# State-space parameters multiplied without zero blocks, placed on the block diagonal by ScalarE, with their last steps spread into the down projection

## Chip, cores and metric

One NeuronCore of a Trainium2 chip. The metric is the device time of one execution in microseconds, the median of several. Engines are named as in the profile: PE (TensorE matmul), PEld (its weight loads), DVE (VectorE), ACT (ScalarE), POOL (GpSimd), SP (SyncE, which here only issues DMAs).

## What is computed

Four transformer-like layers on 256 tokens of 1,024 features, in two blocks of two layers. Every layer is a token mixer and a feed-forward with a depthwise convolution. The third mixer holds a state-space part (S5) whose parameters are made on the chip. The reference, cut to what matters here:

```python
def _conv_ffn(xn, w_up, conv_w, conv_b, w_down):       # layers 1 and 2
    a, gval = jnp.split(xn @ w_up, 2, axis=-1)         # 2 x 2816 columns
    a = depthwise_conv(a, conv_w, width=3) + conv_b
    return (jax.nn.gelu(a) * gval) @ w_down

def s5(u, a_re, a_im, log_dt, b_re, b_im, c_re, c_im, ...):   # in layer 3
    abar = exp((a_re + 1j * a_im) * exp(log_dt))       # 32 groups x 64 states
    bbar = (abar - 1) / (a_re + 1j * a_im) * b         # 32 x 64 x 16
    s_t  = abar * s_(t-1) + bbar @ u_t
    y_t  = Re(c @ s_t) + d * u_t
```

## The kernel before

Activations lie feature-major: a tile has 128 features in the partitions and 256 tokens in the columns. Every large product is made in three passes (`mm3`, L187 to L189): weights and activations are split into a high and a low part, and PE adds high x high, high x low and low x high. So each piece of weights (128x1024) is loaded by SP (`raw`), ACT makes its high part (`whi`, L170) and DVE its low part (`wlo`, L172). Four buffers each of raw, whi and wlo, and four PSUM banks, let them run ahead of PE.

A feed-forward (`ffn`, L514) is an up projection of 22 chunks and a down projection of 8 output tiles. A chunk is 48 matmuls of 256 columns: a tile of a and one of the gate. Behind each chunk stands a chain over four engines: DVE multiplies by the norm's factor (ag, L526), ACT and DVE make the convolution (L531, twice L539), ACT the activation (L541), POOL multiplies by the gate (cv, L542), ACT makes the high part (ah, L543) and POOL the low part (al, L544). The tile cv has two buffers, and ag three. The down projection takes 66 matmuls for an output tile, then DVE adds it to h (L569) and `feed` makes the next norm's operand. In the second feed-forward `feed` is `EdgeNorm.feed` (L582): for every tile POOL makes two sums of squares (L255 or L259 and L262; L585 to L591). PE sums them over the partitions with L275, in its order, after 53 matmuls of the next projection.

The second feed-forward also carries the parameters of the S5 part. `S5.prepare` is a generator that `ffn` gets as `side`; each `next(side)` issues one step, mostly for POOL, behind a chunk's al (L544). Its steps:

- angles, powers, sine and cosine (L659 to L699), on small tiles;
- `times` (L702): one complex product for each of the four powers of B and the four of C, each in two halves (real, imaginary) of three POOL operations (L707, L708, L709) on 128 x 512. A tile has 16 columns for each of its two groups of states, 32 in all, and half of them are zeros: the host has put B and C on a block diagonal (`blocks`);
- the kernel K: 128 small matmuls on PE (L726), then 32 transposes of B (L736), with copies by ACT (L729, L737);
- `turn` (L742): the table E by doubling, from 1 to 64 columns (L753 to L758 on POOL).

After the 22 chunks a loop issues what is left, so all steps are issued ahead of the down projection. The order on each engine is made by a scheduler that sorts by its own estimate of times, and every engine runs its instructions in that order. The parameters arrive by three DMAs from the ACT queue (L640, L643, L645), in the second mixer. In the program E is the tile [128, 2, 16, 64]; its columns 0 to 31 hold B at first, columns 32 to 63 C.

Of the kernel before, what the change touches and what calls it, by code (L numbers as in the profile page):

```python
# [98 lines left out]
def build(tc, A, O, stop=None):  # L99
# [3 lines left out]
    with es:  # L103
# [53 lines left out]
        class Piece:  # L157
            """columns of a weight chunk as high and low part"""
# [42 lines left out]
        def chunkA(src, X, nk=8):  # L201
            """[m 2][k][128] chunk: two feature tiles of X @ W, one bank."""
# [8 lines left out]
        def chunksA(srcs, X, nk=8, late=2, raw=None):  # L211
            """the same for several chunks, where the last operand tiles come late"""
# [23 lines left out]
        class Norm:  # L236
            """RMS norm of the rows of h, as h is made; its gain goes into the operand, 1/rms waits."""
# [30 lines left out]
        def sums(acc, nh, perm=False, more=None, tag="sm"):  # L268
            """token sums of acc over partitions and halves, as columns: [128, 2 (+2)]"""
# [20 lines left out]
        def spread(rs):  # L290
            """columns of token factors -> [128, 256], the same in every partition"""
# [82 lines left out]
        def chunkB(srcs, X, toks, nk=4, n=512, tag="mm"):  # L374
            """token-major: chunks [k][n]; one bank for each token tile"""
# [22 lines left out]
        def qk_head(l, j, X, rb, qkv):  # L398
            """tiles q_j, q_4+j, q_8+j, k_8+j, k_4+j, k_j; all but k_j in order of token parity"""
# [13 lines left out]
        def softmax_rows(s, n):  # L413
            """rows of s (SBUF) -> probabilities, in place"""
# [101 lines left out]
        def ffn(nm, win, cw, cb, wdown, act, shifts, feed, side=None):  # L516
# [6 lines left out]
            for i in range(NF):  # L523
# [21 lines left out]
                if side is not None:  # L545
                    with tc.issue_after(last.ins):
                        for _ in range(1 + (i + 1) % 2):
                            next(side, None)
            for _ in side or ():
                pass  # L550
# [13 lines left out]
            for m in range(8):  # L564
# [5 lines left out]
                feed(m)  # L570

# [60 lines left out]
        class S5:  # L632
            """y = Re(C s), s_t = a s_(t-1) + B~ u_t, four tokens to a step: over quads c of tokens
            s_c = a^4 s_(c-1) + w_c, w_c = sum_j a^(3-j) B~ u_(4c+j). In the frame that turns with the phase of a^4
            the recurrence has the real factor |a|^4: two real scans, z. Then
            y_(4c+j) = Re(C a^(j+1) s_(c-1)) + sum_(i<=j) K_(j-i) u_(4c+i), K_l = Re(C a^l B~)."""

            def __init__(self):
# [3 lines left out]
                self.Bm = self.E[:, :, :, 0:32]  # L642
                nc.scalar.dma_start(out=self.Bm, in_=A["s5_b"])  # L643
                self.C0 = self.E[:, :, :, 32:64]
                nc.scalar.dma_start(out=self.C0, in_=A["s5_c"])  # L645
# [4 lines left out]
            def prepare(self, lbp):  # L650
                """the parameters, in steps that go between other work"""
                P, Bm, C0, C, B, K = self.P, self.Bm, self.C0, self.C, self.B, self.K
# [46 lines left out]
                GS(C0[:, 1], C0[:, 1], -1.0, None, op0=ALU.mult)  # L699
                yield  # L700
                x = lambda c: c.unsqueeze(2).to_broadcast([128, 16, 32])

                def times(o, a, re, im, ops=(ALU.subtract, ALU.add)):
                    """o = a * (re + i im); o, a: real and imaginary [128, 16, 32]"""
                    for c, op in enumerate(ops):
                        tm = sp.tile([128, 512], F32, tag="t%d" % c, name="tm", bufs=1).rearrange("p (a b) -> p a b", a=16)
# [7 lines left out]
                for j in (2, 1, 0):  # L714
                    yield from times(b[j], b[j + 1], are, aim)
# [458 lines left out]
def prepare(inp):  # L1174
# [65 lines left out]
    def blocks(v):  # L1240
# [3 lines left out]
        for g in range(2):  # L1244
            o[g, :, :, g, :] = v[:, g].transpose(1, 0, 2)
# [41 lines left out]
```

## Time and profile before

| | us |
|---|---|
| median of 3 runs (1568.94 to 1570.26) | 1569.27 |
| span of the profiled execution | 1566.8 |
| PE busy | 1519.9 (97%) |
| DVE busy | 1066.2 (68%) |
| ACT busy | 779.6 (50%) |
| POOL busy | 613.3 (39%) |
| DMA, mean of 16 engines | 166 GB/s |

The only time of the profiled execution that is known is its span, from the first to the last instruction; the run's own time also holds what lies around it. PE is busy nearly everywhere, so the places where it is not are to be looked for in the slices and stretches. A busy share is a mean over four layers that are limited by different things.

### The profile page before, as it was taken

The page shows a single profiled execution, that of the slowest core. Times are in us where ns is not written, and L with a number is a line of the kernel's source. Part 1 is how long each engine was busy: PE and PEld are TensorE (multiplying, and loading weights), DVE is VectorE, ACT ScalarE, POOL GpSimd, SP SyncE. Part 2 cuts the span into 40 slices and gives each one's busy share as a digit, 9 for nine tenths or more (in the row PEclk, how much of TensorE's full clock was granted, in tenths as well). Part 3 has the DMA queues.
Part 4 walks back from the last instruction along what each step waited for, and adds up shares of the span by engine and source line. Part 5 has one row for each costly group of instructions (what it writes and reads, how often), then busy time and mean ns, then how long its engine had stood idle before and what let it go on. Part 6 is the DMA issues. An engine that isn't in the chain of part 4 may idle for free.

```text
span 1566.8 us, 30996 instructions
## 1 busy us (share of the span) xinstructions
PE 1519.9 (97%) x12596; PEld 1482.1 (95%) x12596; DVE 1066.2 (68%) x1384; ACT 779.6 (50%) x1192; POOL 613.3 (39%) x606
## 2 busy tenths in 40 slices
PE   9999999999999999999988799999999998999997
PEld 8899999999999999999977799999999997999997
DVE  6756566766666566648587587978766667776754
ACT  4644444555444544445544444456555445565542
POOL 5500023333336000224999984444433312333332
PEclk9999999999999999999999999999999999999999
DMA  8554355555464643565443265335554554355553
GB/s 254 188 181 148 127 176 187 186 187 174 159 208 156 219 163 134 169 195 185 150 136 134 88 196 191 109 115 177 188 188 151 184 181 138 106 182 185 172 161 112
DMA packets 90542, 260.07 MB, mean 166 GB/s; under 512 B 17688, under 2 KB 28840, under 8 KB 90400
## 3 DMA queue, kind: packets, MB, share of 16 engines
q1 hardware_dynamic: 78688, 254.05, 49.4%
q10 hardware_dynamic: 11552, 3.73, 1.1%
q8 instruction: 98, 1.61, 0.4%
q14 instruction: 44, 0.36, 0.1%
q0 software_dynamic: 160, 0.32, 0.1%
HBM read 256.45 MB, written 1.10 MB: 164 GB/s over the span
## 4 chain that ended last, share of the span: by engine, by line
PE 77%; POOL 11%; DVE 7%; issue 2%; DMA 1%; ACT 1%; DVEq 0%; ACTq 0%; POOLq 0%
PE ps_mm L187 24%; PE ps_mm L189 24%; PE ps_mm L188 24%; DVE wlo L172 3%; POOL tm L708 1%; POOL al L544 1%; POOL cv L542 1%; DVE xl L247 1%; PE ps_sm L443 1%; POOL s5c L709 1%; POOL s5b L709 1%; ACT whi L170 1%; DVE h L474 1%; POOL s5b L707 1%; POOL s5c L707 1%
## 5 line engine op out<-in xcount | busy, mean ns | idle before, releaser
L172 DVE TENSOR_TENSOR wlo<-raw,whi 128x1024 fp32r<-128x1024 f32 (+3 forms) x536 | 649.8, 1227 | 275.9 <-ACT whi L170 268.4
L170 ACT CAST whi<-raw 128x1024 fp32r<-128x1024 f32 (+3 forms) x536 | 509.7, 958 | 427.0 <-PE ps_mm L188 342.6
L189 PE MATMUL ps_mm<-xh,wlo 128*128 128x256 f32 x2352 | 671.7, 286 | 14.7 <-DVE wlo L172 14.5
L187 PE MATMUL ps_mm<-xh,whi 128*128 128x256 f32 x2352 | 669.6, 285 | 3.4 <-DVE gate L464 1.7
L188 PE MATMUL ps_mm<-xl,whi 128*128 128x256 f32 x2352 | 670.2, 285 | 0.8 <-DVE xl L247 0.8
L189 PEld LDWEIGHTS ps_mm<-xh,wlo 128*128 128x128 f32 x2352 | 453.4, 193 | 18.2 <-DVE wlo L172 18.2
L187 PEld LDWEIGHTS ps_mm<-xh,whi 128*128 128x128 f32 x2352 | 453.6, 193 | 4.8 <-ACT whi L170 3.5
L188 PEld LDWEIGHTS ps_mm<-xl,whi 128*128 128x128 f32 x2352 | 453.7, 193 | 3.2 <-DVE xl L247 2.9
L189 PE MATMUL ps_mm<-ah,wlo 128*128 128x256 f32 x704 | 199.3, 283 | 1.6 <-DVE wlo L172 1.6
L187 PE MATMUL ps_mm<-ah,whi 128*128 128x256 f32 x704 | 199.3, 283 | 0.6 <-ACT whi L170 0.6
L188 PE MATMUL ps_mm<-al,whi 128*128 128x256 f32 x704 | 199.2, 283 | 0.0
L542 POOL TENSOR_TENSOR cv<-cv,ag 128x256 f32<-128x256 f32 x88 | 115.4, 1312 | 211.8 <-ACT cv L541 191.3
L465 POOL TENSOR_TENSOR gate<-gate 128x256 f32<-128x256 f32 x16 | 20.0, 1258 | 343.3 <-DVE gate L464 343.3
L259 POOL TENSOR_TENSOR sq<-h 128x256 f32<-128x256 f32 (+1 forms) x47 | 70.5, 1499 | 184.7 <-DVE h L569 93.4
L189 PEld LDWEIGHTS ps_mm<-ah,wlo 128*128 128x128 f32 x704 | 135.2, 192 | 1.8 <-DVE wlo L172 1.8
L187 PEld LDWEIGHTS ps_mm<-ah,whi 128*128 128x128 f32 x704 | 135.2, 192 | 0.8 <-ACT whi L170 0.8
L188 PEld LDWEIGHTS ps_mm<-al,whi 128*128 128x128 f32 x704 | 135.2, 192 | 0.0
L539 DVE SCALAR_TENSOR_TENSOR cv<-ag,vec,cv 128x255 f32<-128x255 f32 (+1 forms) x176 | 102.0, 579 | 20.1 <-ACT cv L531 17.1
L543 ACT CAST ah<-cv 128x256 fp32r<-128x256 f32 x88 | 35.8, 407 | 136.3 <-POOL cv L542 136.2
L544 POOL TENSOR_TENSOR al<-cv,ah 128x256 fp32r<-128x256 f32 x88 | 75.4, 857 | 34.6 <-ACT ah L543 34.1
L526 DVE TENSOR_TENSOR ag<-ps_mm,rb 128x512 f32<-128x512 f32 x88 | 60.5, 687 | 40.2 <-PE ps_mm L189 39.8
L531 ACT ACTIVATE cv<-ag,vec 128x256 f32<-128x256 f32 x88 | 52.6, 598 | 26.2 <-POOL al L544 18.9
(342 smaller groups left out, 2127.1 us busy)
## 6 DMA issues: line engine op xcount, KB each, us to landing
raw<-w_up SPq DMA_DIRECT2D x88, 512.0 KB, 3.6
raw<-w_fi SPq DMA_DIRECT2D x88, 512.0 KB, 3.7
raw<-w_qk SPq DMA_DIRECT2D x48, 512.0 KB, 3.6
raw<-w_gate SPq DMA_DIRECT2D x32, 512.0 KB, 3.6
raw<-w_down SPq DMA_DIRECT2D x32, 512.0 KB, 3.5
raw<-w_fo SPq DMA_DIRECT2D x32, 512.0 KB, 3.6
raw<-w_v SPq DMA_DIRECT2D x24, 512.0 KB, 4.5
raw<-w_u SPq DMA_DIRECT2D x16, 512.0 KB, 6.0
```

Of the source, the lines that this page charges most:

```text
L170: nc.scalar.copy(self.hi[:, :n], raw[:, :n])
L172: eng.tensor_tensor(self.lo[:, :n], raw[:, :n], self.hi[:, :n].bitcast(F32), op=ALU.subtract)
L187: nc.tensor.matmul(out, lhsT=a[0], rhs=b[0], start=start, stop=False)
L188: nc.tensor.matmul(out, lhsT=a[0], rhs=b[1], start=False, stop=False)
L189: nc.tensor.matmul(out, lhsT=a[1], rhs=b[0], start=False, stop=stop)
L259: nc.gpsimd.tensor_tensor(q, hs, hs, op=ALU.mult)
L526: nc.vector.tensor_tensor(ag, ps, bc2(rb), op=ALU.mult)
L531: nc.scalar.activation(c, a, AF.Identity, scale=w[j0], bias=cb[:, i:i + 1])
L539: nc.vector.scalar_tensor_tensor(out=c[:, o], in0=a[:, s_], scalar=w[j], in1=c[:, o], op0=ALU.mult, op1=ALU.add)
L542: nc.gpsimd.tensor_tensor(c, c, ag[:, 1, :], op=ALU.mult)
L543: nc.scalar.copy(ah[:, i, :], c)
L544: last = nc.gpsimd.tensor_tensor(al[:, i, :], c, ah[:, i, :].bitcast(F32), op=ALU.subtract)
```

## The change

1. B and C come from the host without their zero blocks: 16 columns for a tile, not 32. Each `times` operation is on 128 x 256. The products stay in two packed buffers (`pk`) that take turns; for C the first operand is `Cp`, columns 0 to 15 of E.
2. `place` copies each half-step's result onto the block diagonal (into B, C0 or C) with two ACT operations on 128 x 256, each multiplied by a column of ones and zeros (`half`) that keeps one group's partitions. A result is placed when the next one has been made. There are 18 placements, 36 ACT instructions.
3. The steps are issued more slowly, 30 of them in the up projection and 5 in the down projection: behind an output tile, as long as m is under 6.

```diff
@@ ffn
-                        for _ in range(1 + (i + 1) % 2):
+                        for _ in range(1 + (i % 3 == 0)):
                             next(side, None)
-            for _ in side or ():
-                pass
...
                 feed(m)
+                if side is not None and m < 6:
+                    next(side, None)
+            for _ in side or ():
+                pass
@@ S5.__init__
-                self.Bm = self.E[:, :, :, 0:32]
-                nc.scalar.dma_start(out=self.Bm, in_=A["s5_b"])
                 self.C0 = self.E[:, :, :, 32:64]
-                nc.scalar.dma_start(out=self.C0, in_=A["s5_c"])
+                self.pk = sp.tile([128, 2, 2, 16, 16], F32, name="s5pk", bufs=1)
+                nc.scalar.dma_start(out=self.pk[:, 0], in_=A["s5_b"])
+                self.Cp = self.E[:, :, :, 0:16]
+                nc.scalar.dma_start(out=self.Cp, in_=A["s5_c"])
+                self.half = sp.tile([128, 2], F32, name="s5h", bufs=1)
+                for g in range(2):
+                    nc.gpsimd.memset(self.half[64 * g:64 * g + 64, g:g + 1], 1.0)
+                    nc.gpsimd.memset(self.half[64 * g:64 * g + 64, 1 - g:2 - g], 0.0)
@@ S5.prepare
-                GS(C0[:, 1], C0[:, 1], -1.0, None, op0=ALU.mult)
+                GS(Cp[:, 1], Cp[:, 1], -1.0, None, op0=ALU.mult)
                 yield
-                x = lambda c: c.unsqueeze(2).to_broadcast([128, 16, 32])
+                x = lambda c: c.unsqueeze(2).to_broadcast([128, 16, 16])
+                late = []
+                def place(dst, v):
+                    late.append((dst, v))
+                    if len(late) > 1:
+                        placed()
+                def placed():
+                    dst, v = late.pop(0)
+                    for g in range(2):
+                        nc.scalar.activation(dst[:, :, 16 * g:16 * g + 16], v, AF.Copy, scale=self.half[:, g:g + 1])
-                def times(o, a, re, im, ops=(ALU.subtract, ALU.add)):
+                def times(dst, o, a, re, im, ops=(ALU.subtract, ALU.add)):
...
                         G2(o[c], a[c], x(re), op=ALU.mult)
                         G2(tm, a[1 - c], x(im), op=ALU.mult)
                         G2(o[c], o[c], tm, op=op)
+                        place(dst[c], o[c])
                         yield
-                yield from times(b[3], [Bm[:, 0], Bm[:, 1]], cr, ci)
+                at, to = two_(pk[:, 0]), two_(pk[:, 1])
+                yield from times(b[3], to, at, cr, ci)
                 for j in (2, 1, 0):
-                    yield from times(b[j], b[j + 1], are, aim)
+                    at, to = to, at
+                    yield from times(b[j], to, at, are, aim)
...
+                while late:
+                    placed()
+                yield
```

Three places show how the rows move. **POOL, in the middle of the up projection**, behind the chunks that carry `times`; cv and al are the chain's, s5b, s5c, s5pk and tm the products', E the first C. Before:

```order
L544 TENSOR_TENSOR al<-cv,ah 128x256
L707 TENSOR_TENSOR s5c<-E,s5p 128x512 x2
L709 TENSOR_TENSOR s5b<-s5b,tm 128x16x32
L542 TENSOR_TENSOR cv<-cv,ag 128x256
L709 TENSOR_TENSOR s5b<-s5b,tm 128x16x32
L542 TENSOR_TENSOR cv<-cv,ag 128x256
L707 TENSOR_TENSOR s5b<-s5b,s5p 128x16x32
L544 TENSOR_TENSOR al<-cv,ah 128x256
L708 TENSOR_TENSOR tm<-s5b,s5p 128x512
L707 TENSOR_TENSOR s5b<-s5b,s5p 128x16x32
L708 TENSOR_TENSOR tm<-s5b,s5p 128x512
```

Now (L728, L729, L730 are the former L707, L708, L709; s5pk are the packed buffers):

```order
L730 TENSOR_TENSOR s5pk<-s5pk,tm 128x256
L542 TENSOR_TENSOR cv<-cv,ag 128x256
L729 TENSOR_TENSOR tm<-s5pk,s5p 128x256
L730 TENSOR_TENSOR s5pk<-s5pk,tm 128x256
L544 TENSOR_TENSOR al<-cv,ah 128x256
L728 TENSOR_TENSOR s5pk<-s5pk,s5p 128x256
L729 TENSOR_TENSOR tm<-s5pk,s5p 128x256
L730 TENSOR_TENSOR s5pk<-s5pk,tm 128x256
L542 TENSOR_TENSOR cv<-cv,ag 128x256
```

Each product's operation has 256 columns for 512, and a chunk's cv stands behind three of them, not behind up to five.

**ACT, at the same chunks.** Before:

```order
L543 CAST ah<-cv 128x256
L170 CAST whi<-raw 128x1024
L541 ACTIVATE cv<-cv 128x256
L170 CAST whi<-raw 128x1024
L531 ACTIVATE cv<-ag,vec 128x256
L170 CAST whi<-raw 128x1024
```

Now (L721 is a placement; s5pk and s5h are its operands):

```order
L541 ACTIVATE cv<-cv 128x256
L721 ACTIVATE s5c<-s5pk,s5h 128x16x16 x2
L170 CAST whi<-raw 128x1024
L543 CAST ah<-cv 128x256
L531 ACTIVATE cv<-ag,vec 128x256
L170 CAST whi<-raw 128x1024
L541 ACTIVATE cv<-cv 128x256
```

In every such chunk a pair of placements stands ahead of a cast of weights and of ah; the pair waits for POOL's L730, and the rest of ACT's queue waits with it.

**POOL, at the end of the up projection.** Before, al's last two rows and the table E:

```order
L754 TENSOR_TENSOR t<-E,s5p 128x256 x2
L758 TENSOR_TENSOR E<-E,t 128x16x16
L542 TENSOR_TENSOR cv<-cv,ag 128x256
L757 TENSOR_TENSOR E<-E,t 128x16x16
L544 TENSOR_TENSOR al<-cv,ah 128x256
L753 TENSOR_TENSOR E<-E,s5p 128x16x32 x2
L754 TENSOR_TENSOR t<-E,s5p 128x512 x2
L758 TENSOR_TENSOR E<-E,t 128x16x32
L757 TENSOR_TENSOR E<-E,t 128x16x32
L255 TENSOR_TENSOR acc<-h 128x256
```

Now, from the last al (L784, L785, L788, L789 are the former L753, L754, L757, L758):

```order
L544 TENSOR_TENSOR al<-cv,ah 128x256
L776 MEMSET E 128x16
L777 MEMSET E 128x16
L784 TENSOR_TENSOR E<-E,s5p 128x16
L785 TENSOR_TENSOR t<-E,s5p 128x16
```

and, with the smaller widths between left out, up to the first tile of the down projection:

```order
L784 TENSOR_TENSOR E<-E,s5p 128x16x16 x2
L785 TENSOR_TENSOR t<-E,s5p 128x256 x2
L789 TENSOR_TENSOR E<-E,t 128x16x16
L788 TENSOR_TENSOR E<-E,t 128x16x16
L784 TENSOR_TENSOR E<-E,s5p 128x16x32 x2
L785 TENSOR_TENSOR t<-E,s5p 128x512
L255 TENSOR_TENSOR acc<-h 128x256
```

Of the table, all 36 operations now stand behind the last al, where before only the widest six did; the first sum of squares (L255) still comes behind nearly all of them. On PE the 128 matmuls for K and the transposes keep their number, as blocks between chunks: K behind chunk 19, the transposes behind K and the last three chunks. The rows of SP are the same.

## Rows read from the trace of the kernel before

**Rows 1.** The page: span, and POOL's busy tenths in 40 slices.
```profile
span 1566.8 us, 30996 instructions
...
POOL 5500023333336000224999984444433312333332
```

**Rows 2.** Timeline of lines (ns min/median/max, starts): first, then second feed-forward.
```profile
L474 DVE SCALAR_TENSOR_TENSOR h<-ps_mm,h x4: 675/677/683, 263.0 to 276.1; 128x512 f32<-128x512 f32 x4
...
L544 POOL TENSOR_TENSOR al<-cv,ah x22: 740/742/1212, 293.7 to 408.0; 128x256 fp32r<-128x256 f32 x22
...
L569 DVE TENSOR_TENSOR h<-ps_mm,h x8: 423/424/425, 417.7 to 465.2; 128x256 f32<-128x256 f32 x8
...
L474 DVE SCALAR_TENSOR_TENSOR h<-ps_mm,h x4: 676/677/681, 708.9 to 722.0; 128x512 f32<-128x512 f32 x4
...
L569 DVE TENSOR_TENSOR h<-ps_mm,h x8: 409/424/425, 903.7 to 950.8; 128x256 f32<-128x256 f32 x8
```

**Rows 3.** Stretches: us; PE, PEld, DVE, ACT, POOL busy (instructions); clock, DMA share, GB/s.
```profile
286.00:410.00 124.00, 124.00 (x1035) 124.00 (x1035) 88.46 (x111) 71.50 (x112) 47.83 (x44) 1.00 0.55 180
738.00:783.00 45.00, 43.91 (x360) 43.09 (x359) 26.80 (x34) 24.11 (x40) 40.09 (x67) 1.00 0.45 153
783.00:897.00 114.00, 93.22 (x817) 88.72 (x815) 79.33 (x70) 50.27 (x83) 114.00 (x110) 0.94 0.37 122
897.00:951.00 54.00, 52.29 (x433) 52.09 (x434) 43.70 (x43) 25.59 (x37) 46.43 (x41) 1.00 0.62 196
```

**Rows 4.** Waits from 738 to 898 us (total, times, longest).
```profile
ACT ah L543 <- POOL cv L542: 45.7, 21, 5.6
...
PE ps_aux L726 <- POOL s5c L709: 6.7, 1, 6.7
```

**Rows 5.** POOL from 738 to 898 us: L707, L708, L709.
```profile
738.00:898.00 160.00, 19.73 (x16) 0.96 0.39 130
...
738.00:898.00 160.00, 22.97 (x16) 0.96 0.39 130
...
738.00:898.00 160.00, 24.31 (x16) 0.96 0.39 130
```

**Rows 6.** Groups of POOL, 700 to 960 us (busy us, mean ns).
```profile
L544 POOL TENSOR_TENSOR al<-cv,ah 128x256 fp32r<-128x256 f32 x22 | 24.6, 1117 | 0.5 <-ACT ah L543 0.5
...
L542 POOL TENSOR_TENSOR cv<-cv,ag 128x256 f32<-128x256 f32 x22 | 22.7, 1035 | 10.3 <-PE ps_mm L189 10.2
...
L753 POOL TENSOR_TENSOR E<-E,s5p 128x256 f32<-128x256 f32 x2 | 1.2, 616 | 0.0
```

**Rows 7.** POOL in order of time: single operations (start us, us).
```profile
801.67 1.71 POOL L542 TENSOR_TENSOR cv<-cv,ag 128x256 f32<-128x256 f32 x1
...
807.50 1.05 POOL L707 TENSOR_TENSOR s5b<-s5b,s5p 128x512 f32<-128x512 f32 x1
...
885.95 0.74 POOL L542 TENSOR_TENSOR cv<-cv,ag 128x256 f32<-128x256 f32 x1
```

**Rows 8.** Timeline of L246: ScalarE with a factor for each partition, 128x256.
```profile
L246 ACT ACTIVATE xh<-h,vec x8: 495/504/512, 709.6 to 723.2; 128x256 fp32r<-128x256 f32 x8
```

**Rows 9.** PE in order of time: L726 and L736 (start us, us).
```profile
869.41 0.55 PE L726 MATMUL ps_aux<-s5c,s5b 128*32 128x96 f32 x8
...
871.50 0.66 PE L736 MATMUL ps_aux<-ident,s5b 128*128 128x128 f32 x4
...
875.48 1.47 PE L736 MATMUL ps_aux<-ident,s5b 128*128 128x128 f32 x12
```

**Rows 10.** POOL by stretch: operations with tile E, then all.
```profile
875.00:908.00 33.00, 23.99 (x38) 1.00 0.38 115
...
907.00:951.00 44.00, 36.43 (x35) 1.00 0.66 208
```

**Rows 11.** In order of time: POOL's last L262, PE's first L275.
```profile
954.63 0.73 POOL L262 TENSOR_TENSOR acc<-acc,sq 128x256 f32<-128x256 f32 x1
...
956.91 0.50 PE L275 MATMUL ps_sm<-ones,acc 128*128 128x1 f32 x4
```

More of the change, by code (lines that the diff above doesn't have):

```diff
@@ L650, in prepare @@
             def prepare(self, lbp):
-                P, Bm, C0, C, B, K = self.P, self.Bm, self.C0, self.C, self.B, self.K
+                P, C0, C, B, K, pk, Cp = self.P, self.C0, self.C, self.B, self.K, self.pk, self.Cp
                 ar, ai, ld, dt, rho, t0, t1, xr, den, cr, ci, two, are, aim, rho4 = [P[:, i, :] for i in range(15)]
@@ L698, in prepare @@
                 G2(ci, ci, den, op=ALU.mult)
-                GS(C0[:, 1], C0[:, 1], -1.0, None, op0=ALU.mult)
+                GS(Cp[:, 1], Cp[:, 1], -1.0, None, op0=ALU.mult)
                 yield
-                x = lambda c: c.unsqueeze(2).to_broadcast([128, 16, 32])
-                def times(o, a, re, im, ops=(ALU.subtract, ALU.add)):
+                x = lambda c: c.unsqueeze(2).to_broadcast([128, 16, 16])
[9 more added lines that the diff above has]
+                def times(dst, o, a, re, im, ops=(ALU.subtract, ALU.add)):
                     for c, op in enumerate(ops):
-                        tm = sp.tile([128, 512], F32, tag="t%d" % c, name="tm", bufs=1).rearrange("p (a b) -> p a b", a=16)
+                        tm = sp.tile([128, 512], F32, tag="t%d" % c, name="tm", bufs=1)[:, :256] \
+                            .rearrange("p (a b) -> p a b", a=16)
                         G2(o[c], a[c], x(re), op=ALU.mult)
@@ L709, in times @@
                         G2(o[c], o[c], tm, op=op)
+                        place(dst[c], o[c])
                         yield
+                two_ = lambda t: [t[:, 0], t[:, 1]]
                 b = [[B[:, c, :, j, :] for c in range(2)] for j in range(4)]
-                yield from times(b[3], [Bm[:, 0], Bm[:, 1]], cr, ci)
+                at, to = two_(pk[:, 0]), two_(pk[:, 1])
+                yield from times(b[3], to, at, cr, ci)
                 for j in (2, 1, 0):
-                    yield from times(b[j], b[j + 1], are, aim)
-                cc = [[C0[:, 0], C0[:, 1]]] + [[C[:, j, c] for c in range(2)] for j in range(4)]
-                for j in range(4):
-                    yield from times(cc[j + 1], cc[j], are, aim, (ALU.add, ALU.subtract))
+                    at, to = to, at
+                    yield from times(b[j], to, at, are, aim)
+                at, to = two_(Cp), two_(pk[:, 1])
+                for c in range(2):
+                    place(C0[:, c], at[c])
+                for j in range(4):
+                    yield from times(two_(C[:, j]), to, at, are, aim, (ALU.add, ALU.subtract))
+                    at, to = to, (two_(pk[:, 0]) if j == 0 else at)
+                while late:
+                    placed()
+                yield
                 ps = bank("aux")
@@ L1240, in blocks @@
     def blocks(v):
-        o = np.zeros((2, 64, 16, 2, 16), np.float32)
-        v = v.reshape(16, 2, 64, 16)
-        for g in range(2):
-            o[g, :, :, g, :] = v[:, g].transpose(1, 0, 2)
-        return o.reshape(128, 16, 32)
+        return v.reshape(16, 128, 16).transpose(1, 0, 2)
     A["s5_b"] = np.stack([blocks(f("s5_b_re_2")[0]), blocks(f("s5_b_im_2")[0])], axis=1)
```

## Prediction

> **What bounds the kernel now.** The page comes first: POOL, at two to four tenths in the other feed-forwards, stands at nine tenths from the 20th to the 23rd slice, in the second feed-forward [rows 1]. The timeline of single lines says what that stage costs. From the first addition to h ahead of it (L474) to the last one in it (L569) the first feed-forward, which carries no parameters, takes 465.2 - 263.0 = 202.2 us; the second takes 950.8 - 708.9 = 241.9 us [rows 2]. The work on weights and activations is the same, so the parameters cost 39.7 us, and the change can give back no more than that.
>
> The stretches say where. In the first up projection PE is never idle (124 of 124 us). In the second it is busy for 43.9 of 45 us while POOL makes the angles, then for 93.2 of 114 us, in which POOL is busy all the time, and for 52.3 of 54 us behind it; the granted clock falls to 0.94 on the mean of the middle stretch [rows 3]. The waits say how POOL holds PE, which reads nothing of POOL's for a chunk: ACT's ah waits 45.7 us in 21 pieces for POOL's cv, with the casts of weights behind it in ACT's queue [rows 4]. PE waits once for POOL directly: 6.7 us at the K matmuls [rows 4]. So the limit in this stage is POOL's queue, and elsewhere PE.
>
> **What is removed.** The 48 `times` operations take 19.7 + 23.0 + 24.3 = 67.0 us, 1.40 us each [rows 5]; alone, such an operation takes 1.05 us [rows 7]. So 0.35 us of each is contention with another engine. The chain's cv and al, (24.6 + 22.7) / 44 = 1.08 us each [rows 6], take 0.74 us alone and 1.71 us at worst [rows 7]: 0.34 us of contention again.
>
> **What the half-width operations cost.** The nearest row is the table's L753, which writes 256 strided columns too: 0.62 us [rows 6]. The chain's 128x256 at 0.74 us is the upper end. A third of the operations (L730) have two full operands, like the chain's, so I take 32 x 0.62 + 16 x 0.74 = 31.7 us alone, where it was 48 x 1.05 = 50.4.
>
> **Is POOL still too slow?** In the new order the 48 operations stand between the chain's operations of about 11 chunks. A chunk is 48 matmuls of 124 / 1035 = 0.12 us, 5.75 us, so PE needs 63 us for the eleven [rows 3]. POOL needs, alone, 31.7 + 22 x 0.74 = 48 us; with 0.34 us of contention for each of its 70 operations, 72 us. By the first figure it is 15 us ahead, by the second 9 us late. I take the second, since PE at full rate keeps DVE as busy as in the stretch it comes from. But four buffers of whi and wlo are two chunks of lead, and the last four chunks carry the chain alone (2.2 of 5.75 us), where POOL catches up. K, behind chunk 19, must wait for the last product and its placement. I charge 6 us of idle PE, with 0 and 14 as ends.
>
> **What is added on ACT.** 36 placements; the nearest row is the cast of h with a factor for each partition, 0.504 us at 128x256 [rows 8], so 18 us. In the eleven chunks ACT needs 71.5 / 124 x 63 = 36 us [rows 3] and 32 x 0.504 = 16 us more: 52 of 63 us. Hidden, at nothing, as long as a placement does not wait long for POOL; behind it stand the casts of weights, for which DVE and PE wait. POOL in its turn may not overwrite a packed buffer that ACT has not placed yet; there are two steps between, so no charge. The two placements that the order puts in the second mixer follow C's DMA by about as much as before another cast did; none to 2 us, none charged.
>
> **PE's own share** stays: 96 of the 128 K matmuls took 871.50 - 869.41 = 2.1 us, so 2.8 for all; 12 transposes 1.47 us, so 3.9 for 32 [rows 9]. 6.7 us.
>
> **What is moved.** The table E costs POOL 24.0 us [rows 10], and nearly all of it now stands behind the last al. Take the first feed-forward's times as the new ones: the last al ends at 408.7, the last h at 465.2 [rows 2]. POOL then works on E until 432.7 and on seven tiles' sums of squares, 36.4 us [rows 10], until 469.1: 3.9 us behind the last h. Before, the last sum was there 955.4 - 950.8 = 4.6 us behind the last h, and PE asked for it at 6.1 us [rows 2, 11]. Now it comes at 3.9 + 4.6 = 8.5 us, and PE stands 2.4 us at L275, with everything behind it in its queue. E's operations ran while DVE had little to do; with 0.1 us of contention for each of 36 it is 6 us. I take 4, with 0 and 8 as ends. The three DMAs keep their places in ACT's queue and carry half the bytes; SP's and POOL's queues of DMAs are not passed by anything. The four memsets and the two 128x4 operations of DVE that change places: nothing.
>
> **Sum**, against the span of 1566.8 us [rows 1]: - 39.7 + 6.7 (PE) + 6 (POOL late) + 4 (sums) = 1543.8. The median of the runs stands 2.5 us above that span: **1546 us**, a gain of 23.
>
> **Rivals.**
> 1. *POOL keeps up everywhere.* The contention falls as POOL has less to do, the lead hides the rest, and the table ends in time. Then only PE's own 6.7 us are left: 1566.8 - 39.7 + 6.7 + 2.5 = 1536 us. For it: alone POOL needs 48 of 63 us. Against it: 0.34 us a piece was there on operations of 256 columns too.
> 2. *POOL and DVE exclude each other.* The two levels of the same operation, 0.74 and 1.71 us [rows 7], look like waiting for a whole operation of another engine. If no POOL operation could run beside one of DVE, a chunk would need DVE's 88.5 / 124 x 5.75 = 4.1 us [rows 3] and POOL's 48 / 11 = 4.4 us: 8.5 us, in eleven chunks 30 us more than PE. Then 1546 - 6 + 30 = 1570, no change. Against it: in the first feed-forward DVE is busy 71% and POOL 39% of a stretch in which PE never waits [rows 3]; the mean of 0.34 us is far from the whole. Part of the way, 1555 to 1565, is more likely.
> The Trainium skill states this rule (SBUF — State Buffer, section Who interferes with whom): a VectorE instruction with two SBUF inputs and a GpSimd instruction that reads SBUF take one shared port, as a lock for the whole instruction. By the rule alone the sum would be the 1570 of this rival; by the rows' means it is the 1546 above.
> 3. *ACT becomes the queue that everything waits in* (slower). Each of the 16 pairs of placements among the eleven chunks stands ahead of casts of weights and waits for a POOL operation. ACT has 63 - 52 = 11 us to spare; beyond 0.7 us of wait a pair, PE pays. ACT's waits for cv are 45.7 / 21 = 2.2 us now [rows 4]. From 16w - 11 = 39.7 - 6.7 - 4 = 29, so w = 2.5 us, the kernel is slower than before; at 3.0 us a pair the loss is 37 us: 1566.8 - 39.7 + 6.7 + 37 + 4 + 2.5 = 1577 us. Against it: the placement comes one half-step late, so POOL has mostly finished.
> 4. *The narrow operations are hardly shorter*, which would be a change that doesn't do what it says: POOL stays at 1.4 us each, the table alone is moved, 24 us, for 16 us of ACT. That ends where rival 2 does. Against it: 0.62 us [rows 6].
>
> **How the numbers follow.** A measurement of this kernel tells about 0.2%, 3 us, from no change. Forecast (1540 to 1554) 0.57; rival 1 0.20; rivals 2 and 4 0.18, of which 0.15 faster and 0.03 within 3 us; rival 3 0.05, of which 0.04 slower and 0.01 the same. Faster 0.92, the same 0.04, slower 0.04. The range takes in rival 1, 1535 with a little less of PE's share, and above, both late terms at their ends: 1546 + 8 + 4 = 1558. About 0.15 lies outside.
>
> **What would show it.** Right: from L474 to the last L569 about 215 us; L728 to L730 at 0.9 to 1.0 us; POOL idle at the last four chunks; L275 waiting for L262 for 2 to 6 us; ACT's wait for cv well under 45.7 us. Wrong: PE idle for more than 15 us between chunks 8 and 19; waits of L721 for L730 over 0.7 us a pair; products near 1.4 us; or a granted clock that stays below 1.00 for more than a few us.

## The result, and the profile after

The changed kernel takes 1555.45 us (median of 4 runs, 1554.38 to 1556.42) where the kernel before takes 1569.11: a ratio of 0.9913, 95% interval 0.9901 to 0.9925. It gains 13.7 us; 23 were forecast, and 1555.45 lies inside the range of 1535 to 1558, near its upper end. The page's span and POOL's slices, to be read beside [rows 1]:

```profile
span 1552.4 us, 31045 instructions
...
POOL 6500023433326000124998694435333312333332
```

The four nines in a row in POOL's 20th to 23rd slice became 9, 9, 8 and 6. The timeline of the two lines that bound the second feed-forward, beside [rows 2] (L567 is the former L569):

```profile
L474 DVE SCALAR_TENSOR_TENSOR h<-ps_mm,h x4: 675/678/683, 708.1 to 721.2; 128x512 f32<-128x512 f32 x4
```
```profile
L567 DVE TENSOR_TENSOR h<-ps_mm,h x8: 409/424/425, 888.8 to 936.4; 128x256 f32<-128x256 f32 x8
```

The stage takes 936.4 - 708.1 = 228.3 us, 13.6 less than the 241.9 of before and 26.1 more than the first feed-forward, which again takes 202.2. So 13.6 of the 14.4 us between the two spans are gained in this stage, and the forecast of about 215 us for it was missed by 13. The stretches, beside [rows 3] (us; PE, PEld, DVE, ACT, POOL busy; clock, DMA share, GB/s):

```profile
738.00:783.00 45.00, 43.49 (x359) 42.88 (x358) 28.70 (x36) 25.41 (x40) 42.11 (x69) 1.00 0.48 156
783.00:860.00 77.00, 66.00 (x609) 62.32 (x608) 50.60 (x52) 47.58 (x88) 65.80 (x68) 0.96 0.42 140
783.00:897.00 114.00, 103.00 (x914) 99.32 (x913) 74.86 (x81) 69.51 (x123) 91.46 (x110) 0.97 0.43 141
897.00:937.00 40.00, 40.00 (x336) 40.00 (x335) 31.14 (x33) 19.13 (x26) 39.77 (x37) 1.00 0.65 208
```

PE's idle time is all ahead of 860, where the products are: 11 us of 77. There no engine is full: POOL has 11 us idle as well, ACT and DVE far more. (The mean clock of 0.96 comes of two pieces of 3.4 us, from 789.7 and from 857.9 us, in which the granted clock is 0.50, the lower level of 1.2 GHz. PE had paused ahead of each: for 1.4 and 1.2 us between 785.8 and 788.9, and for 2.3 us from 854.8.) The waits from 738 to 898 us, beside [rows 4]:

```profile
ACT ah L543 <- POOL cv L542: 12.7, 8, 3.3
ACT s5c L721 <- POOL s5pk L730: 12.5, 7, 2.3
...
POOL al L544 <- ACT ah L543: 11.7, 13, 1.7
...
PE ps_mm L189 <- DVE wlo L172: 8.0, 10, 1.3
ACT s5b L721 <- POOL s5pk L730: 6.7, 5, 2.0
```

ACT's wait for cv fell from 45.7 to 12.7 us, and 12.5 + 6.7 = 19.2 us of waits of placements for products are new. The products' own time, beside [rows 5] (L728, L729, L730 over the same stretch):

```profile
738.00:898.00 160.00, 14.29 (x16) 0.98 0.45 146
```
```profile
738.00:898.00 160.00, 15.06 (x16) 0.98 0.45 146
```
```profile
738.00:898.00 160.00, 20.21 (x16) 0.98 0.45 146
```

That is 49.6 us for 67.0, 1.03 us each. At the end, POOL's last L262 and PE's first L275, beside [rows 11]:

```profile
941.41 0.73 POOL L262 TENSOR_TENSOR acc<-acc,sq 128x256 f32<-128x256 f32 x1
```
```profile
942.51 0.50 PE L275 MATMUL ps_sm<-ones,acc 128*128 128x1 f32 x4
```

The sum is there at 942.14, before PE comes to it at 942.51, 6.1 us behind the last h as before. Nothing is lost there.

What is left to explain: 26.1 us of excess are 6.7 of PE's own and 19.4 lost, where 6 were charged.

### The profile page after: what moved, and what is told of

Its sections match the earlier page's. It is cut to its first block, busy times and chain, and to the rows that moved or that the text cites. A ratio compares the mean times of both kernels' runs of the same rounds, so it can differ in the third digit from the quotient of the medians.

```text
span 1552.4 us, 31045 instructions
## 1 busy us (share of the span) xinstructions
PE 1516.7 (98%) x12596; PEld 1479.0 (95%) x12596; DVE 1049.8 (68%) x1384; ACT 794.9 (51%) x1228; POOL 585.8 (38%) x610
## 4 chain that ended last, share of the span: by engine, by line
PE 80%; POOL 8%; DVE 7%; issue 2%; ACT 2%; DMA 1%; DVEq 0%; ACTq 0%; POOLq 0%
PE ps_mm L187 25%; PE ps_mm L188 25%; PE ps_mm L189 25%; DVE wlo L172 3%; POOL s5pk L730 1%; DVE xl L247 1%; POOL al L544 1%; PE ps_sm L443 1%; POOL tm L729 1%; POOL s5pk L728 1%; ACT whi L170 1%; DVE h L474 1%; PE ps_mm L1108 1%; POOL sq L259 0%; POOL cv L542 0%
## 5 line engine op out<-in xcount | busy, mean ns | idle before, releaser
L172 DVE TENSOR_TENSOR wlo<-raw,whi 128x1024 fp32r<-128x1024 f32 (+3 forms) x536 | 638.1, 1205 | 279.8 <-ACT whi L170 270.8
L189 PEld LDWEIGHTS ps_mm<-xh,wlo 128*128 128x128 f32 x2352 | 453.1, 193 | 12.7 <-DVE wlo L172 12.7
L542 POOL TENSOR_TENSOR cv<-cv,ag 128x256 f32<-128x256 f32 x88 | 109.2, 1241 | 222.4 <-ACT cv L541 202.0
L539 DVE SCALAR_TENSOR_TENSOR cv<-ag,vec,cv 128x255 f32<-128x255 f32 (+1 forms) x176 | 95.9, 545 | 17.2 <-ACT cv L531 14.2
L465 POOL TENSOR_TENSOR gate<-gate 128x256 f32<-128x256 f32 x16 | 19.4, 1225 | 203.1 <-DVE gate L464 203.1
L262 POOL TENSOR_TENSOR acc<-acc,sq 128x256 f32<-128x256 f32 x57 | 58.2, 1022 | 3.9
```

The lines of the kernel that those rows point to most:

```text
L172: eng.tensor_tensor(self.lo[:, :n], raw[:, :n], self.hi[:, :n].bitcast(F32), op=ALU.subtract)
L189: nc.tensor.matmul(out, lhsT=a[1], rhs=b[0], start=False, stop=stop)
L262: nc.gpsimd.tensor_tensor(acc, acc if k0 + i > 1 or n == 1 else q[:, 0, :], q[:, i, :], op=ALU.add)
L539: nc.vector.scalar_tensor_tensor(out=c[:, o], in0=a[:, s_], scalar=w[j], in1=c[:, o], op0=ALU.mult, op1=ALU.add)
L542: nc.gpsimd.tensor_tensor(c, c, ag[:, 1, :], op=ALU.mult)
```

## The experiments

Each ratio is to runs of the kernel before on the same chip. "Stage" is the time from the first L474 to the last h, as above.

| kernel | products on POOL | stage, us | time, us | ratio to before, interval |
|---|---|---|---|---|
| before | full width | 241.9 | 1569.1 | |
| the change | packed | 228.3 | 1555.5 | 0.9913 (0.9901 to 0.9925) |
| e3 | packed, old pacing | 227.2 | 1552.7 | 0.9902 (0.9886 to 0.9918) |
| e4 | full width, new pacing | 238.8 | 1567.3 | 0.9991 (0.9981 to 1.0001) |
| e1 | packed, placements behind ah | 226.9 | 1553.9 | 0.9912 (0.9895 to 0.9930) |
| e2 | packed, no placements | 227.9 | 1561.7 | 0.9959 (0.9943 to 0.9975) |
| e10 | packed, between cv and al | 228.2 | 1555.8 | 0.9909 (0.9889 to 0.9929) |
| e12 | packed, placements wait for none | 230.1 | 1557.9 | 0.9923 (0.9904 to 0.9942) |
| e8 | packed, one step a chunk | 220.9 | 1548.6 | 0.9869 (0.9852 to 0.9885) |
| e6 | none | 209.8 | 1538.1 | 0.9805 (0.9790 to 0.9819) |
| e5 | memsets, 0.95 us | 210.8 | 1540.7 | 0.9827 (0.9812 to 0.9841) |
| e11 | memsets, 1.17 us | 214.7 | 1541.5 | 0.9823 (0.9802 to 0.9843) |
| e7 | none, they are on DVE | 214.9 | 1542.2 | 0.9830 (0.9815 to 0.9845) |
| e9 | none, on DVE, one step a chunk | 220.1 | 1546.7 | 0.9853 (0.9833 to 0.9873) |

### Which part of the change gains: e3 and e4

e3 keeps packing and placements and goes back to the old pacing; e4 keeps the new pacing with the old full-width products.

```diff
-                        for _ in range(1 + (i % 3 == 0)):
+                        for _ in range(1 + (i + 1) % 2):
                             next(side, None)
+            for _ in side or ():
+                pass
...
-                if side is not None and m < 6:
-                    next(side, None)
-            for _ in side or ():
-                pass
```

> Edit: parts 1 and 2 of the change alone (packed products, placements), with the steps issued as in the kernel before, all of them ahead of the down projection. Theory A: the same taking of turns, with 16 us more of POOL's work (most of the table) back in the up projection, of which the last chunks without products hide a part: 1555 to 1563 us. Theory B: POOL's work decides, 1563 to 1569 us.

> Edit: part 3 of the change alone: full-width products straight into the block diagonal, no placements, but 30 steps in the up projection and the rest in the down projection. POOL was busy all the time before, and about 14 us of the table leave the up projection: both theories 1555 to 1561 us. If the pacing gives nothing, 1567 to 1570 us.

The packing alone gives all of the gain (1552.7 us, faster than either theory said), the pacing alone none that can be told (1567.3, and the interval holds 1); of e4's expectation the last sentence came true, not the range of both theories.

### Do ACT's waits for the products cost it: e1, e2, e12

e1 holds each pair of placements behind the chunk's ah in ACT's queue; e2 leaves the placements out; e12 lets them copy data that are long there.

```diff
# e1
-                nc.scalar.copy(ah[:, i, :], c)
+                side_ah[0] = nc.scalar.copy(ah[:, i, :], c)
...
+                    with tc.issue_after(side_ah[0].ins):
                         for g in range(2):
                             nc.scalar.activation(dst[:, :, 16 * g:16 * g + 16], v, AF.Copy, scale=self.half[:, g:g + 1])
# e2
+                nc.gpsimd.memset(self.B, 0.0)
+                nc.gpsimd.memset(self.C, 0.0)
+                nc.gpsimd.memset(self.C0, 0.0)
...
-                    for g in range(2):
-                        nc.scalar.activation(dst[:, :, 16 * g:16 * g + 16], v, AF.Copy, scale=self.half[:, g:g + 1])
# e12
-                        place(dst[c], o[c])
+                        place(dst[c], Cp[:, c])
```

> Edit: in ACT's queue each pair of placements gets an ordering edge behind the high part (ah) of the chunk behind which it was issued; POOL's work is unchanged. Theory A (the order in ACT's queue: a pair that stands ahead of ah waits for L730, and then POOL waits for ah, so ACT and POOL take turns): ACT's waits for L730 fall from 19 us to under 4, POOL's waits for ah from 12 us to under 4, from the first addition to h (L474) to the last (L567) it takes 212 to 220 us instead of 228, and the time is 1540 to 1548 us. Theory B (POOL and DVE slow each other, so POOL's products are the limit wherever the pairs stand): the waits move to other rows and the time stays within 1552 to 1557 us.

> Edit: the 36 placements are left out (B, C and the first C hold zeros, set by POOL in the second mixer), so the state-space part of the third mixer gives nothing but the skip term; POOL makes the same products. Theory A: about as e1, a little faster because ACT also has 18 us less work: 1538 to 1546 us. Theory B: no more than 3 us faster than the changed kernel, 1552 to 1556 us. If ACT's work itself, and not its waits, is the limit, e2 is at least 6 us faster than e1.

> As the change, with all 48 products on POOL, but the placements copy other data that have long been there, so ACT never waits for a product; the placed parameters are wrong. Against the kernels with memsets, whose placements did not wait for POOL either, the only difference is that POOL's 48 operations read two operands. Theory B (POOL reading against DVE reading): the loss stays, stage 225 to 229 us, time 1551 to 1556 us. Theory F (the memsets were faster because no placement waited for them): stage 212 to 216 us, time 1539 to 1545 us.

The waits of placements for products are gone in e2 and e12 and down from 19.2 to 6.3 us in e1, and the stage stays at 227 to 230 us in all three. e1's time is within theory B's range; e12 is 1 us over B's range for the stage and 2 us over the one for the time. e1's and then e12's waits of ACT:

```profile
ACT ah L543 <- POOL cv L542: 27.5, 15, 3.3
```
```profile
ACT ah L543 <- POOL cv L542: 35.0, 16, 4.4
```

Only the name of the wait changes: what ACT doesn't wait for at L721 it waits for at ah. So the theory that the order in ACT's queue costs the 13 us falls. (e2's time, 1561.7 us, lies outside every range that was expected: its memsets of the empty tiles stood in the mixer, and the stage began 7 us later. The last section shows it.)

### Does POOL's queue cost it: e10

```diff
-                nc.gpsimd.tensor_tensor(c, c, ag[:, 1, :], op=ALU.mult)
+                last = nc.gpsimd.tensor_tensor(c, c, ag[:, 1, :], op=ALU.mult)
                 nc.scalar.copy(ah[:, i, :], c)
-                last = nc.gpsimd.tensor_tensor(al[:, i, :], c, ah[:, i, :].bitcast(F32), op=ALU.subtract)
                 if side is not None:
...
+                nc.gpsimd.tensor_tensor(al[:, i, :], c, ah[:, i, :].bitcast(F32), op=ALU.subtract)
```

> As the change, but in the program the steps stand between a chunk's cv and its al, so POOL has products to do while ACT makes ah. Theory D (POOL's turn: 5.98 us busy for a chunk and 0.97 us idle for ACT's round trip, 6.95 us where PE needs 5.75): the idle time goes, 11 chunks get 0.9 us shorter, the stage falls from 228.3 to 217 to 220 us, the time to 1543 to 1547 us. Theory B (contention): products and DVE's operations overlap as before, stage 225 to 230 us, time 1552 to 1557 us.

POOL's wait for ah fell from 11.7 to 2.6 us, and the stage is the same 228.2. Filling POOL's gaps gains nothing: theory D falls.

### Does it matter what POOL does in that time: e6, e5, e11

e6 leaves the 48 products out; e5 and e11 put memsets in their places, shorter and longer than the products' mean of 1.03 us (`C3` stands for 1024 or 1280 columns of C).

```diff
-                        G2(o[c], a[c], x(re), op=ALU.mult)
-                        G2(tm, a[1 - c], x(im), op=ALU.mult)
-                        G2(o[c], o[c], tm, op=op)
-                        place(dst[c], o[c])
+                        for _ in range(3):
+                            nc.gpsimd.memset(C3, 0.0)
+                        place(dst[c], pk[:, 0, c])
```

> The 48 products of L728 to L730 are left out altogether; the placements copy other data, all else stays. It gives the floor that the products stand on. Both theories B and C: POOL is free for cv and al, the stage falls from 228.3 to 209 to 213 us (202.2 of the first feed-forward + 6.7 of PE's own matmuls and transposes), the time to 1536 to 1540 us. If the stage stays above 220, the loss is not the products' at all but that of the first steps (angles) or of the placements, K and transposes.

> The 48 products of L728 to L730 are replaced, one for one and in the same places of POOL's queue, by memsets of 128x1024 (by the 1.17 us of the 128x1280 memset before, an estimate of 0.95 us each; the products took 1.03 us in the mean). So the parameters are not multiplied, and the placements copy other data. POOL is held as long as before, but reads nothing. Theory B (POOL's two-operand products and DVE's two-operand subtractions and convolutions make each other longer): DVE's wlo falls from 1397 ns in the mean to some 1250, the second feed-forward (first L474 to last L567) from 228.3 to 213 to 217 us, the time to some 1541 to 1544 us. Theory C (no matter how long they are made, products stand in POOL's queue ahead of the cv and al of a chunk, so ACT and the weight casts behind it wait): the stage stays at 224 to 229 us, the time at 1552 to 1556 us.

> As the kernel with memsets in place of the 48 products, but each of 128x1280, 1.17 us by the row of before, so POOL is held longer than the products hold it (56 us for 49.6), while it reads nothing. Parameters are not multiplied. Theory D: POOL's turn for a chunk of four is 4 x 1.17 + 1.7 busy and 0.9 idle, 7.3 us: the loss is that of the change or more, stage 228 to 235 us, time 1554 to 1562 us. Theory B: DVE is not slowed, its wlo stays near 1200 ns, POOL is late by at most (4 x 1.17 + 1.7 - 5.75) x 12 = 7 us, of which the buffers ahead take some: stage 211 to 218 us, time 1539 to 1545 us.

The stretch 783 to 860 of e6, e11 and, beside them, e12, whose placements are as free of POOL as theirs:

```profile
783.00:860.00 77.00, 76.61 (x744) 76.13 (x743) 51.05 (x68) 47.85 (x78) 26.44 (x30) 1.00 0.55 175
```
```profile
783.00:860.00 77.00, 73.33 (x666) 71.83 (x667) 56.63 (x68) 44.49 (x73) 75.88 (x83) 1.00 0.52 166
```
```profile
783.00:860.00 77.00, 69.26 (x635) 66.55 (x635) 53.44 (x54) 40.61 (x62) 70.10 (x83) 0.98 0.46 151
```

In e11 POOL is fuller than in any run with packed products, 75.9 of 77 us, and ACT waits 33.3 us for cv; yet PE works 73.3 us and the stage is 15.4 us shorter than e12's. POOL's 48 operations read two operands in e12 and none in e11.

One more thing tells these two apart. In e5, e6, e11 and e12 placements move ahead into the mixer, since nothing holds them: 30, 34, 28 and 18 of the 36. e12's other 18 stand close together on ACT from 771.6 to 781.6 us, and PE waits there for a cast of weights:

```profile
772.00:782.00 10.00, 5.76 (x41) 5.31 (x40) 3.45 (x5) 9.98 (x23) 4.13 (x9) 0.83 0.31 102
```

PE pauses once for 3.7 us, and for 3.4 us behind that the granted clock is 0.50: some 5 of the 15 us are this block's, by an estimate from these two. e2 has the products and no placement at all, and its stage of 227.9 us is 13.2 longer than e11's. So 10 to 13 us go with the reading of operands. The mechanism of theory B stands. Its sizes do less well: e11 came within its range, e5's stage (210.8 us) was 2 us shorter than it said.

### How the reading costs it

Two engines side by side for one chunk of the change, DVE first, then POOL, then ACT (start us, us):

```profile
828.55 1.71 DVE L539 SCALAR_TENSOR_TENSOR cv<-ag,vec,cv 128x255 f32<-128x255 f32 x2
830.19 1.64 DVE L172 TENSOR_TENSOR wlo<-raw,whi 128x1024 fp32r<-128x1024 f32 x1
831.76 0.68 DVE L526 TENSOR_TENSOR ag<-ps_mm,rb 128x512 f32<-128x512 f32 x1
834.34 1.23 DVE L172 TENSOR_TENSOR wlo<-raw,whi 128x1024 fp32r<-128x1024 f32 x1 [1.91 <-ACT whi L170]
```
```profile
829.19 0.80 POOL L728 TENSOR_TENSOR s5pk<-s5pk,s5p 128x256 f32<-128x256 f32 x1
829.95 0.80 POOL L729 TENSOR_TENSOR tm<-s5pk,s5p 128x256 f32<-128x256 f32 x1
830.83 1.60 POOL L730 TENSOR_TENSOR s5pk<-s5pk,tm 128x256 f32<-128x256 f32 x1
832.39 0.74 POOL L542 TENSOR_TENSOR cv<-cv,ag 128x256 f32<-128x256 f32 x1
834.69 1.47 POOL L544 TENSOR_TENSOR al<-cv,ah 128x256 fp32r<-128x256 f32 x1 [1.57 <-ACT ah L543]
836.12 0.80 POOL L728 TENSOR_TENSOR s5pk<-s5pk,s5p 128x256 f32<-128x256 f32 x1
```
```profile
832.46 0.91 ACT L721 ACTIVATE s5c<-s5pk,s5h 128x256 f32<-128x256 f32 x2 [1.68 <-POOL s5pk L730]
833.28 1.03 ACT L170 CAST whi<-raw 128x1024 fp32r<-128x1024 f32 x1
```

Follow the ends. POOL's L729 ends at 830.75; wlo, begun at 830.19, ends 1.08 us after that, at 831.83. L730, begun at 830.83, ends 0.60 us after wlo, at 832.43. al, begun at 834.69 beside the next wlo, ends 0.59 us after it. It is so all through the stretch from 783 to 860: wherever two such operations of POOL and DVE overlap, the later one ends a fixed time behind the earlier, a wlo 1.08 or 1.09 us (15 times), an L730, cv or al 0.58 to 0.60 (19), an L728 or L729 0.48 (21), an L539 0.28 or 0.29 (19). Each waits for the whole of the other's operation, and both count the wait as busy. DVE's ag, with one operand in PSUM, runs its usual 0.68 us beside L730. Then both stand idle for some 1.2 us, because ACT could only place, and cast the next weights, when L730 had ended. From L728 to L728 it is 6.93 us; PE needs 5.75.

The same in e11, DVE then POOL:

```profile
827.77 0.48 DVE L539 SCALAR_TENSOR_TENSOR cv<-ag,vec,cv 128x255 f32<-128x255 f32 x1
828.17 1.22 DVE L172 TENSOR_TENSOR wlo<-raw,whi 128x1024 fp32r<-128x1024 f32 x1
829.31 0.68 DVE L526 TENSOR_TENSOR ag<-ps_mm,rb 128x512 f32<-128x512 f32 x1
829.91 1.69 DVE L172 TENSOR_TENSOR wlo<-raw,whi 128x1024 fp32r<-128x1024 f32 x1
```
```profile
826.19 3.62 POOL L729 MEMSET s5c<- 128x1280 f32 x3
829.79 0.73 POOL L542 TENSOR_TENSOR cv<-cv,ag 128x256 f32<-128x256 f32 x1
830.46 1.16 POOL L729 MEMSET s5c<- 128x1280 f32 x1
```

The wlo at 828.17 runs beside memsets in 1.22 us; the one at 829.91 meets POOL's cv and ends 1.08 us after it, at 831.60; the memset beside it takes its 1.16 us. The Trainium skill states just this (SBUF — State Buffer, section Who interferes with whom): a VectorE instruction with two SBUF inputs contends with a GpSimd instruction that reads SBUF, not with one that only writes, and the port that they share is an exclusive lock. These rows agree.

How much of the stage that takes can be counted. From start to start and undisturbed, wlo takes 829.31 - 828.17 = 1.14 us and L539 0.40 in the rows above. POOL's, in order of time in the change:

```profile
784.46 1.43 POOL L730 TENSOR_TENSOR s5pk<-s5pk,tm 128x256 f32<-128x256 f32 x2
785.85 0.72 POOL L544 TENSOR_TENSOR al<-cv,ah 128x256 fp32r<-128x256 f32 x1
786.54 0.61 POOL L728 TENSOR_TENSOR s5pk<-s5pk,s5p 128x256 f32<-128x256 f32 x1
787.12 0.61 POOL L729 TENSOR_TENSOR tm<-s5pk,s5p 128x256 f32<-128x256 f32 x1
```

L730 takes 0.70 us, al (and so cv) 0.69, L728 (and so L729) 0.58. Between 783 and 860 the change runs 20 wlo, 22 L539, 29 of L728 and L729, 16 L730 and 23 of cv and al: 22.8 + 8.8 + 16.8 + 11.2 + 15.9 = 75.5 of 77 us, though neither engine alone is full. The 23 of cv and al are 11.5 chunks, so that is 6.6 us for each, where PE needs 5.75. It is an upper measure: the same count in e8 gives 81 of 77. Counted by what an operation still takes when the other has ended (1.08, 0.28, 0.48 and 0.59 us, as above) it is 20 x 1.08 + 22 x 0.28 + 29 x 0.48 + 39 x 0.59 = 64.7 us. The two engines are not one full queue, either: in 8.0 of the 77 us both stand idle, as for 1.2 us in the chunk above. So the exclusion makes each round from DVE over ACT to POOL and back longer, and the rest of the loss is these rounds' waiting; how the 77 us divide between the two was not measured.

### Less of it at a time, and none of it: e8, e7, e9

e8 takes one step behind every chunk, where the change takes two behind every third chunk and one behind the others; then it takes two behind each tile of the down projection, where the change takes one. e7 gives the 48 products to DVE. e9 does both.

```diff
# e8
-                        for _ in range(1 + (i % 3 == 0)):
+                        for _ in range(1):
                             next(side, None)
...
-                if side is not None and m < 6:
+                for _ in range(2 if side is not None else 0):
                     next(side, None)
# e7, and so for all three products
-                        G2(o[c], a[c], x(re), op=ALU.mult)
+                        nc.vector.tensor_tensor(o[c], a[c], x(re), op=ALU.mult)
```

> One step of the preparation behind every chunk of the up projection, in place of one or two; what is left goes two steps at a time behind the tiles of the down projection. So never more than three products stand between two chunks on POOL, and the last ones come at the up projection's end. Theory B: each product still meets DVE's operations, the loss is the same: stage 226 to 230 us, time 1553 to 1557 us. Theory C, in the form that a chunk with six products and its own cv and al (6 x 1.03 + 2.2 = 8.4 us) is longer than PE's 5.75 us while one with three (5.3 us) is not: stage 214 to 219 us, and unless the squares of the down projection end late behind E's operations, the time 1541 to 1546 us.

> The 48 products run on DVE instead of POOL, nothing else is changed. DVE gets 48 instructions of 0.4 to 0.5 us each, some 22 us, in a stretch in which it was busy 51 of 77 us. Theory B (the pair slows each other): the pairs of POOL and DVE are gone, but DVE becomes nearly full; wlo falls to some 1270 ns, the stage to 217 to 222 us, the time to 1545 to 1550 us. Theory C (products ahead of cv and al in POOL's queue): POOL's queue is free, products stand ahead of weight subtractions instead, up to 1.4 us at a time, and these have buffers ahead: stage 211 to 215 us, time 1538 to 1542 us.

> The 48 products on DVE and one step of the preparation behind every chunk, the two edits of the runs that were faster than the change, together. Theory B (POOL's products and DVE's operations on two SBUF operands make each other longer): on DVE the products have no pair, so their density matters little; what is left above the floor of 1538.1 us without products is 2 to 4 us for DVE's queue: 1538 to 1542 us. Theory D (POOL's turn for a chunk, with the idle time for ACT's ah between cv and al, is longer than PE's 5.75 us): POOL has no products in either, the same. If the time is over 1545 us, the late K matmuls and transposes in the down projection cost by themselves.

e8's stage is 7.4 us shorter than the change's, between what B and C expected: a chunk with three products always is nearer to fitting than one with six every third time, and theory B was wrong that their spacing wouldn't matter. e7 is the fastest kernel that does the whole work, 1542.2 us. Its stage, 214.9 us, is within theory C's figure and below B's, so e7 and e8 alone would speak for a long queue on POOL; what speaks against it is e11, where that queue is longer still. e7's stretch, and two of its DVE rows with the POOL row beside them:

```profile
783.00:860.00 77.00, 74.44 (x723) 73.33 (x724) 70.65 (x110) 57.34 (x105) 31.93 (x27) 1.00 0.51 166
```
```profile
830.21 0.41 DVE L730 TENSOR_TENSOR s5pk<-s5pk,tm 128x256 f32<-128x256 f32 x1
830.55 1.22 DVE L172 TENSOR_TENSOR wlo<-raw,whi 128x1024 fp32r<-128x1024 f32 x1
```
```profile
830.82 1.54 POOL L542 TENSOR_TENSOR cv<-cv,ag 128x256 f32<-128x256 f32 x1 [2.34 <-ACT cv L541]
```

On DVE a product takes 0.34 us from start to start, for 0.58 to 0.70 on POOL. cv still waits for wlo, but POOL has time for that. The shared count is 26 x 1.14 + 26 x 0.40 + 44 x 0.34 + 27 x 0.69 = 73.6 us for 13.5 chunks, 5.5 each: under PE's 5.75.

e9 missed its 1538 to 1542, by 5 us: the two edits don't add up. The expectation would have put that down to K's matmuls and transposes, which now run from 881.3 to 898.7 us, in the down projection. The trace does not: from 877 to 931 PE is busy 54.0 of 54 us at a clock of 1.00. What PE loses between 860 and 897, 2.3 us where e7 loses none, it loses by 864, before wlo and whi, and the granted clock is then 0.50 for 3.4 us from 865.2. What e9 has there and e7 has not is POOL's table E: 32 of its 36 operations run between 808.7 and 860 us among the chunks, where in e7 the first starts at 867.3, behind the last al. One of them, which overlaps a wlo that ends at 853.40:

```profile
852.28 1.72 POOL L789 TENSOR_TENSOR E<-E,t 128x256 f32<-128x256 f32 x1
```

It ends 0.60 us after the wlo, as the products did. So the table among the chunks is the likely reason that e9 is slower than e7; no run tests that by itself. e8 has the table among the chunks as well, from 842.3, so its spreading may be worth more than its 7 us show.

## Why the prediction was right, and where not

The sum was 1566.8 - 39.7 + 6.7 + 6 + 4 = 1543.8, for a span that came out at 1552.4. That the time lies inside the range is luck in part: the term for POOL went 5.4 us over its own upper end, and the term for the sums, charged at 4, was 0.

- **What can be given back, - 39.7, and PE's own 6.7**: right. Without products (e6) the stage takes 209.8 us, 7.6 more than the first feed-forward.
- **The products, 31.7 us alone and 0.34 of contention on each**: right. L728 takes 0.61 alone, L730 0.72; the 48 took 49.6 us where 31.7 + 48 x 0.34 = 48.0 were worked out.
- **POOL late, 6 us (0 to 14)**: this is the term that failed. It is 228.3 - 202.2 - 6.7 = 19.4 us, over its upper end, and e6 puts 228.3 - 209.8 = 18.5 of it down to the products. (PE's idle time in the stage, 13.0 us for e6's 2.4, and half of the 6.8 us at the lower clock show 14 of them; the others lie where PE counts as busy.) The step reckoned POOL's 72 us against PE's 63 and let the four buffers and the last chunks give most of the 9 us back. It charged the contention to POOL and left DVE's share out. e11 holds POOL longer and loses 214.7 - 209.8 = 4.9 us against e6's floor, e2, with the products and no placements, 227.9 - 209.8 = 18.1: a long queue on POOL is what the buffers do take up, the exclusion is not. POOL was not late by its own work, either: it is idle for 11 of the 77 us. Reckoned as one queue of both engines, the upper measure is 75.5 us for 11.5 chunks that take PE 66.
- **Rival 2, the exclusion**: the mechanism that decided, and the part of the way that it named, 1555 to 1565, is where the time fell, a little above the forecast's own 1540 to 1554. It got a chance of 0.18 together with rival 4, which was too low. Its full price, 8.5 us a chunk and 1570, was too high: DVE's 4.1 us held ag, which doesn't meet POOL's operations (0.68 us), and waits for POOL. By the undisturbed times DVE has 2 x 1.14 + 2 x 0.40 = 3.1, and with POOL's 4.4 that makes 7.5; the chunk above took 6.93. What was brought against it, that POOL and DVE are busy 39% and 71% side by side in the first feed-forward, is no argument: by the undisturbed times a chunk there asks for 2 x 1.14 + 2 x 0.40 + 2 x 0.69 = 4.5 of its 5.75 us from the shared queue, which fits.
- **ACT**: the placements took 0.49 to 0.51 us, as forecast. Rival 3's wait came: 19.2 us over 16 pairs is 1.2 us a pair, by its formula 16 x 1.2 - 11 = 8 us of loss. It cost nothing that could be measured: e1 and e12 take the wait away and stay within 3 us. The formula took ACT's queue for the limit, and ACT was busy 47.6 of 77 us.
- **The sums, 4 us (0 to 8)**: 0. POOL's table and feeds ended 5.7 us behind the last h, not 8.5, and PE comes at 6.1.
- With the two terms as measured: 1566.8 - 39.7 + 6.7 + 19.4 + 0 = 1553.2; the stage also began 0.8 us earlier, at 708.1 for 708.9.

Of the signs named for right, the products near 1.0 us, ACT's short wait for cv and POOL's idle time at the last chunks (it is busy 8.7 of the 20 us from 860 to 880) came, the stage of 215 us and PE's wait at L275 did not. Of the signs for wrong, the pairs' wait over 0.7 us came, and a granted clock of 0.96 over 77 us; PE's idle time from 738 to 860 is 12.5 us, short of the 15.

## What to carry to other kernels

Where GpSimd and VectorE both run operations on two SBUF operands, add up what both have to do in one stretch, undisturbed, as if they were one queue, and compare that with the bound engine's time. A sum under it fitted here (4.5 and 5.5 of 5.75 us a chunk); a sum over it (6.6) went with a loss, though the sum is an upper measure and not the time itself. The busy shares of each engine hide this, since they hold the waits. A wait that is taken away tells nothing until the stage gets shorter: three edits here (e1, e2, e12) took a wait of ACT's away and each time another had its length. Short element-wise work that collides on GpSimd may be cheaper on a VectorE that is already busy: here 48 products on it gave 13 us more than the change alone.

## What was not expected

A memset of POOL's can hold up DVE after all, where DVE runs another form of operation. In e2, three memsets of the tiles that its placements no longer fill stood in the mixer. POOL's rows, then DVE's:

```profile
647.80 3.52 POOL L657 MEMSET s5b<- 128x4096 f32 x1
651.25 3.52 POOL L658 MEMSET s5c<- 128x4096 f32 x1
654.70 0.96 POOL L659 MEMSET E<- 128x1024 f32 x1
```
```profile
650.10 5.58 DVE L851 TENSOR_SCALAR lbp<-lbp 128x4 f32<-128x4 f32 x1
652.04 3.66 DVE L172 TENSOR_TENSOR wlo<-raw,whi 128x1024 fp32r<-128x1024 f32 x3
```

The same tensor_scalar in the change, without the memsets:

```profile
649.89 0.16 DVE L850 TENSOR_SCALAR lbp<-lbp 128x4 f32<-128x4 f32 x1
```

In e2 it began at 650.10 and ended at 655.68, with the last of three memsets without a gap (655.66). The seven DVE instructions behind it, L852, three of L464 and three wlo, began at their usual distances, and all of them ended with it, by 655.70; PE is busy for 0.2 of the 6 us from 650 to 656, and the whole mixer ended 7 us later. In e11 the memsets stood beside two-operand subtractions and cost those nothing, and in e2 the wlo at 648.96, beside the first memset, took its usual 1.23 us. So what a memset blocks seems to depend on the form of DVE's operation, and POOL didn't give way between two of its own. The Trainium skill, in the section named above, has tensor_scalar among the forms that can take the shared pair of ports; that such a short one waits out several of POOL's is what these rows add. It was seen this once; other forms were not tried.
